# Placing the weights of the last w_o product, the FFN's first sums and a table load elsewhere around an RMS norm

## The chip, the cores and the metric

The kernel runs on one core of one Trainium2 chip. The metric is the device time of one execution in microseconds (us). A core has five engines with a queue each: TensorE (PE: matrix products and transposes, into PSUM), VectorE (DVE), ScalarE (ACT), GpSimd (POOL), and SyncE (SP), which here issues most DMA transfers. An engine takes its instructions in the order in which they were written or scheduled; where one waits, all behind it on that engine wait too.

## The reference

One block of a streaming encoder on 512 tokens of 1024 features, in float32 (the FFN has 2816 inner columns). Only the part from the gated merge to the FFN's start concerns the change:

```python
h = h + (g_a * ya + g_b * yb) @ w_o[l]
hn = rmsnorm(h, norm_ffn_g[l])      # xf * rsqrt(mean(xf * xf) + EPS) * g
gu = hn @ w_ffn_in[l]
g, up = jnp.split(gu, 2, axis=-1)
h = h + (jax.nn.silu(g) * up) @ w_ffn_out[l]
```

## The kernel before, in words

Every float32 operand of a product is split into a high and a low part (`split`, L80: ACT copies the rounded high part, DVE subtracts it for the low part), and a product is three matmuls (`mm3`, L74 to L78: high x high, high x low, low x high). So each weight tile costs a DMA into a raw tile, one ACT and one DVE instruction, before TensorE can use it.

The product with w_o is done by Strassen's scheme (Winograd's form) in seven products of half size, each in two steps u = 0, 1 over the inner dimension (`h_multiply`, L874). Their order is a11 x b11, a12 x b21, s1 x t1, s2 x t2, s4 x b22 (the fifth), s3 x t3, a22 x t4 (the last). The right sides b and t are blocks of w_o and sums of them (the sums were stored in DRAM earlier); `blocks_wo` (L816) loads and splits the two tiles of one side, and `wo_part` (L805) chooses the pool. Weight tiles lie in rings: `wop` has four places of tag `whl`, `wp` four of its own, and the raw tiles use three places of `wp`, taken in turn. A tile that takes a place waits until all readers of the place's tile before it are through; a raw place is free when the DVE half of its split has ended. Before the change t1 and t2 lie in `wp` and all other sides in `wop`, so that t4 takes the places of b22.

The fifth product is done for one tile of 128 tokens after the other. Behind each one stands the norm: `finish_h` (L900) adds the product to h (DVE), squares it with a sum along the row (ACT, then a small reduce on DVE), and `scaled` (L339) takes the root (ACT), the reciprocal (DVE) and scales the row (DVE, tile `xs_ffn`). `turned` (L345) transposes two token tiles at a time on TensorE (`pt_ffn`), and ACT and DVE write the high and low part (`hn`) and a plain copy (`x32`) out of PSUM. hn00 and hn10 are the features of tokens 0 to 255, hn01 and hn11 those of tokens 256 to 511. The first pair of FFN column blocks, fg0 and fu0, is multiplied plainly (`project_part`), first with tokens 0 to 255, then with the rest. All later pairs (fg2, fu2, ...) go through Strassen's scheme as well: `weight_sums` (L159) loads a block's two halves and forms four sums of its quarters on DVE (L173 to L176, tiles s21 and s34), which are then split. For fg2 this is begun ahead: the sums s21 and s34, and the split of s21; the raw halves are loaded a second time for the rest.

The order on TensorE is written out by hand from the first product to the end of fg0 and fu0 with the first tokens (`manual_schedule`). The order on all other engines is set by a scheduler, which follows the order of the code where dependences leave a choice, and its own estimate of when each operand is ready. It puts each DMA where its place becomes free.

Which ACT functions are loaded is a table: a root behind other functions needs a table load in front of it, which is an ACT instruction of its own. L945 takes a root of a constant into `warm` to have the table early.

Of the kernel before, what the change touches and what calls it, by code (L numbers as in the profile page):

```python
# [36 lines left out]
def block_kernel(ctx: ExitStack, tc: tile.TileContext, x, norm_mix_g, w_in, b_merge, rel_table,  # L37
# [42 lines left out]
    def split(hi, lo, src):  # L80

        act.activation(hi, src, AF.Copy)  # L82
        dve.tensor_sub(lo, src, f(hi))  # L83
# [161 lines left out]
    def weights(name, ahead=1):  # L245
        prefetch(index[name] + 1 + ahead)
        return made[index[name]]
# [555 lines left out]
    wo = {}  # L803

    def wo_part(name, src):  # L805

        raw = wp.tile([P, 2, S], F32, tag="raw", bufs=3, name=f"raw_{name}")
        sp.dma_start(out=raw[:], in_=src)
        pl = wp if 4 <= len(wo) < 8 else wop
        hl = pl.tile([P, 2, 2, S], F32R, tag="whl", bufs=4, name=f"whl_{name}")  # L810
        split_pair(hl, raw[:])
        wo[name] = hl
# [31 lines left out]
    for j in range(KT):  # L844
        if j >= 4 and j % 2 == 0:
            blocks_wo(("b11", "b21")[j // 2 - 2])
        py = mm_tile(f"po_ya{j}")
        project(py, weights(f"ya{j - j % 2}"), j % 2, aT)
        dve.scalar_tensor_tensor(ta[j], ta[j], 1.0, py[:], ALU.add, ALU.mult)
        dve.tensor_add(ta[j], ta[j], zB[j])  # L850
        at = lo_half if j % 4 < 2 else slice(0, S)
        split(mT[j][:, 0, at], mT[j][:, 1, at], ta[j][:, at])
        if j % 4 == 3:
            m_sum("s1", j // 4)
            m_split("s1", j // 4)
            for name in ("s2", "s4", "s3"):
                m_sum(name, j // 4)
# [25 lines left out]
    def h_read(half, cc, into, tokens=range(2)):  # L883
        for i in tokens:
            hs = ht[2 * into[0] + i][:, into[1] * S:(into[1] + 1) * S]
            dve.scalar_tensor_tensor(hs, bank_of(2 * half + i, cc)[:], 0.5, hs, ALU.mult, ALU.add)
# [17 lines left out]
    with tc.manual_schedule(engines={mybir.EngineType.PE}):  # L904
        h_multiply("a11", "b11", 1, 0, True)
        for u in range(2):
            m_split("s2", u)
        h_read(1, 0, (0, 0))
        h_multiply("a12", "b21", 0, 0, True)
        for t in range(2):  # L910
            finish_h(t, 0, False)
        for u in range(2):
            m_split("s4", u)
        blocks_wo("t3")
        h_multiply("s1", "t1", 0, 1, True)
        for u in range(2):
            m_split("s3", u)
        h_read(0, 1, (1, 1))
        h_multiply("s2", "t2", 1, 0, False)
        h_read(1, 0, (0, 1))  # L920
        blocks_wo("t4")
    aw_stack.close()
    qk_stack.close()
    rnn_stack.close()
# [17 lines left out]
    def hn_at(k, part, half):  # L942
        return bl[k // 4, half][:, part, k % 4]

    act.activation(warm[:], eps_t[:], AF.Sqrt)  # L945
    weight_sums("fg2", True)
    def project_part(o, name, c, half, ks):
        at = slice(c * P, (c + 1) * P)
        whl = weights(name, 0)
# [5 lines left out]
    ends = range(0, KT // 2), range(KT // 2, KT)  # L955
    with tc.manual_schedule(engines={mybir.EngineType.PE}):
        xs = []
        for t in range(2):
            h_multiply("s4", "b22", 0, 1, False, (t,))
            finish_h(t, 1, True)  # L960
            xs.append(scaled(x32p, ht, hsq, "ffn", t)[0])
        weights("fg0")
        h_multiply("s3", "t3", 1, 0, False, us=(0,))
        h_multiply("s3", "t3", 1, 0, False, (0,), us=(1,))
        for jp in (0, 2):
# [5 lines left out]
        for u, jp in ((0, 4), (1, 6)):  # L971
            h_multiply("a22", "t4", 1, 0, False, (0,), us=(u,))
            turned(xs, jp, gf, hn_at, 0, "ffn", f_at)
        finish_h(2, 0, True)
        xs = [scaled(x32p, ht, hsq, "ffn", 2)[0]]
        h_multiply("a22", "t4", 1, 0, False, (1,))
        finish_h(3, 0, True)
# [2 lines left out]
        for name, c in (("fg0", 0), ("fg0", 1), ("fu0", 0), ("fu0", 1)):  # L980
# [8 lines left out]
            project_part(first[-1], name, c, 0, ends[1])  # L989
            if (name, c) == ("fg0", 1):  # L990
                turned(xs, 4, gf, hn_at, 1, "ffn", f_at)
    wo_stack.close()
    xn_stack.close()

# [299 lines left out]
```

## Time and profile before

| | us |
|---|---|
| median of 3 runs (868.69 to 869.67) | 869.65 |
| profiled execution | 871.49 |
| its span | 869.7 |
| TensorE busy | 851.7 (98%) |
| DVE busy | 632.4 (73%) |
| ACT busy | 505.5 (58%) |
| from the fifth product of w_o (497.8) to the first Strassen product of the FFN (551.4) | 53.6 |
| TensorE idle in 500 to 530 | 6.56 |

All times in the rows are counted from the span's start. In a timeline row the first number is the start, the second the duration, and a bracket at the end names the idle time of the engine ahead of the row and what ended it. A row that stands for several instructions (x2, x8) has their number behind it. [...]

### The profile page before, as it was taken

The numbers are of one execution on the slowest core, as the hardware profiler recorded it, in microseconds if no ns is written. First come the engines' busy times: TensorE is split into PE (matmuls) and PEld (weight loads), VectorE is DVE, ScalarE is ACT, GpSimd is POOL, SyncE is SP. The second block draws the span as 40 slices with busy tenths as digits, with TensorE's granted clock in tenths as the row PEclk, the third lists the DMA queues.
The fourth block names the chain that finished last, engine by engine and source line by source line (L and its number), as shares of the span: only waits on it lengthen the run. The fifth ranks groups of instructions, "written<-read, shape, count | busy, mean of one in ns | idle before, by whom it ended". The sixth has DMA issues, their size and how long they took to land.

```text
span 869.7 us, 13005 instructions
## 1 busy us (share of the span) xinstructions
PE 851.7 (98%) x4896; PEld 746.2 (86%) x4896; DVE 632.4 (73%) x973; ACT 505.5 (58%) x869; POOL 97.8 (11%) x135
## 2 busy tenths in 40 slices
PE   8999999999999999999999979999999999999996
PEld 6977887888888888888888868999999999988885
DVE  5789776646666656566558887899888886498973
ACT  7577687641466666567543474565655655474544
POOL 2013312200122222222200000000000001000011
PEclk9999999999999999999999999999999999999999
DMA  8585323339842223242246450747434333394602
GB/s 270 185 300 170 97 73 107 114 107 348 271 129 65 73 66 92 73 122 62 73 145 205 159 165 30 268 145 277 136 115 129 98 97 94 101 323 138 197 20 96
DMA packets 95838, 124.68 MB, mean 143 GB/s; under 512 B 6432, under 2 KB 71568, under 8 KB 95776
## 3 DMA queue, kind: packets, MB, share of 16 engines
q1 hardware_dynamic: 92096, 116.19, 41.0%
q10 hardware_dynamic: 3680, 7.67, 3.1%
q8 instruction: 38, 0.62, 0.3%
q14 instruction: 24, 0.20, 0.1%
HBM read 109.12 MB, written 14.72 MB: 142 GB/s over the span
## 4 chain that ended last, share of the span: by engine, by line
PE 93%; DMA 2%; DVE 2%; ACT 2%; issue 1%; DVEq 0%; ACTq 0%
PE po_out L78 4%; PE po_out L77 4%; PE po_out L76 4%; PE o L749 2%; PE p_fu L77 2%; PE p_fg L77 2%; PE p_fu L78 2%; PE p_fg L78 2%; PE p_fg L76 2%; PE p_fu L76 2%; PE pT L729 2%; PE po_ga L76 2%; PE po_v L76 2%; PE po_q L76 2%; PE po_ga L78 2%; PE po_k L76 2%
## 5 line engine op out<-in xcount | busy, mean ns | idle before, releaser
L718 POOL TENSOR_SCALAR p<-p,rl 128x128 f32<-128x128 f32 (+1 forms) x64 | 39.6, 637 | 165.4 <-DVE rl L716 165.3
L715 ACT ACTIVATE p<-p,m 128x128 f32<-128x128 f32 (+1 forms) x64 | 35.8, 562 | 14.4 <-DVE m L714 14.4
L1057 POOL TENSOR_TENSOR act_lo<-act,act_hi 128x1024 fp32r<-128x1024 f32 x1 | 2.4, 2427 | 306.4 <-ACT act_hi L1056 306.4
L83 DVE TENSOR_TENSOR pp<-pT,pp 128x384 fp32r<-128x384 f32 (+1 forms) x48 | 27.8, 595 | 9.8 <-ACT pp L82 9.7
L83 DVE TENSOR_TENSOR whl_t<-raw_t,whl_t 128x1024 fp32r<-128x1024 f32 x24 | 29.3, 1219 | 4.1 <-ACT whl_t L82 4.1
L714 DVE CUSTOM_DVE_ANT_0 p<-s,bias 128x128 f32<-128x128 f32 (+1 forms) x64 | 29.2, 483 | 3.9 <-PE s L711 3.8
L83 DVE TENSOR_TENSOR whl_qk<-raw_qk,whl_qk 128x1024 fp32r<-128x1024 f32 x16 | 21.5, 1345 | 11.3 <-ACT whl_qk L82 11.3
L82 ACT ACTIVATE whl_t<-raw_t 128x1024 fp32r<-128x1024 f32 x24 | 25.1, 1049 | 6.8 <-PE po_out L78 4.0
L76 PE MATMUL po_gr<-xnT,whl_gr 128*128 128x512 f32 (+1 forms) x80 | 28.1, 352 | 0.1
L597 DVE TENSOR_TENSOR spillf<-spillf,spillf 128x1024 f32<-128x1024 f32 x16 | 19.5, 1221 | 11.7 <-DMA spillf<-in_w_ffn_out_dram 11.7
L77 PE MATMUL po_xr<-xnT,whl_xr 128*128 128x512 f32 (+1 forms) x80 | 27.8, 353 | 0.1
L77 PE MATMUL po_gr<-xnT,whl_gr 128*128 128x512 f32 (+1 forms) x80 | 27.8, 348 | 0.0
L78 PE MATMUL po_gr<-xnT,whl_gr 128*128 128x512 f32 (+1 forms) x80 | 27.5, 348 | 0.0
L83 DVE TENSOR_TENSOR whl_fg_s<-s_fg,whl_fg_s 128x1024 fp32r<-128x1024 f32 x20 | 24.3, 1222 | 4.3 <-ACT whl_fg_s L82 4.3
L78 PE MATMUL po_xr<-xnT,whl_xr 128*128 128x512 f32 (+1 forms) x80 | 27.4, 347 | 0.0
L76 PE MATMUL po_xr<-xnT,whl_xr 128*128 128x512 f32 (+1 forms) x80 | 26.7, 353 | 0.6 <-ACT xnT L353 0.6
L83 DVE TENSOR_TENSOR whl_b<-raw_b,whl_b 128x1024 fp32r<-128x1024 f32 x18 | 21.9, 1218 | 6.6 <-ACT whl_b L82 6.4
L83 DVE TENSOR_TENSOR whl_fu_s<-s_fu,whl_fu_s 128x1024 fp32r<-128x1024 f32 x20 | 24.3, 1222 | 3.1 <-ACT whl_fu_s L82 3.1
L82 ACT ACTIVATE whl_qk<-raw_qk 128x1024 fp32r<-128x1024 f32 x16 | 16.8, 1052 | 16.0 <-PE po_yb L78 8.8
L82 ACT ACTIVATE whl_b<-raw_b 128x1024 fp32r<-128x1024 f32 x18 | 18.9, 1051 | 12.1 <-DMA raw_b<-in_w_o_dram 11.5
L76 PE MATMUL po_gb<-xnT,whl_gb 128*128 128x512 f32 x64 | 25.1, 393 | 0.5 <-DVE sp_p L452 0.3
L76 PE MATMUL po_ga<-xnT,whl_ga 128*128 128x512 f32 x64 | 25.3, 396 | 0.0
(386 smaller groups left out, 3259.4 us busy)
## 6 DMA issues: line engine op xcount, KB each, us to landing
raw_fg<-in_w_ffn_in_dram SPq DMA_DIRECT2D x24, 512.0 KB, 3.9
raw_fu<-in_w_ffn_in_dram SPq DMA_DIRECT2D x22, 512.0 KB, 3.6
raw_qk<-in_w_in_dram SPq DMA_DIRECT2D x32, 256.0 KB, 3.3
spillf<-in_w_ffn_out_dram SPq DMA_DIRECT2D x16, 512.0 KB, 7.3
sums<-spillf SPq DMA_DIRECT2D x16, 512.0 KB, 4.3
raw_t<-sums SPq DMA_DIRECT2D x16, 512.0 KB, 4.4
raw_b<-in_w_ffn_out_dram SPq DMA_DIRECT2D x12, 512.0 KB, 3.5
raw_xr<-in_w_in_dram SPq DMA_DIRECT2D x8, 512.0 KB, 4.6
```

The lines of the kernel that those rows point to most:

```text
L76: pe.matmul(o, sh, mh, start=start, stop=False, skip_group_check=parts)
L77: pe.matmul(o, sh, ml, start=False, stop=False, skip_group_check=parts)
L78: pe.matmul(o, sl, mh, start=False, stop=stop, skip_group_check=parts)
L82: act.activation(hi, src, AF.Copy)
L83: dve.tensor_sub(lo, src, f(hi))
L597: dve.tensor_sub(out_, a_, b_)
L714: dve.tensor_tensor_reduce(prob[qb][:], scs[qb], bias[:, S - w:S], -1.0, 3e38, ALU.add, ALU.min, nmax[:, qb:qb + 1])
L715: act.activation(prob[qb][:], prob[qb][:], AF.Exp, bias=nmax[:, qb:qb + 1], scale=-1.0, accum_out=lsum[:, qb:qb + 1])
L718: pool.tensor_scalar(prob[qb][:], prob[qb][:], rl[:, qb:qb + 1], 1.0, ALU.mult, ALU.mult)
L729: pe.transpose(pt[:, at * P:(at + 1) * P], prob[qb][:, kb * P:(kb + 1) * P], ident[:])
L749: pe.matmul(po[:, S - n:S], st, pp[i][:, part, lo:lo + n], start=kb == 0 and part == 0, stop=kb == NT - 1 and part == 1)
L1057: (pool if i == 0 else dve).tensor_sub(lo[:], o[:], f(hi[:]))
```

## The change

It makes four edits. The sides t1, t2 and t4 now lie in `wp`, the sides b11, b21, b22 and t3 in `wop`, so that t4 takes the places of t1, fg0 those of t2, and fu0 those of t4. t4 is loaded and split ahead of the read of the fourth product, and fg0 ahead of the fifth product; fu0 is asked for behind the read of the last product's first half, where before both came behind the fifth product. The sums of fg2 are asked for behind the transposes of the second tokens, no longer ahead of the fifth product. And the root that loads the table now depends on the fifth tile of the merged branches (`ta[4]`) and stands behind it.

```diff
@@ wo_part
-        pl = wp if 4 <= len(wo) < 8 else wop
+        pl = wp if name[:2] in ("t1", "t2", "t4") else wop
@@ the merge of the branches, tile j
         split(mT[j][:, 0, at], mT[j][:, 1, at], ta[j][:, at])
+        if j == 4:
+            act.activation(warm[:], ta[4][:, 0:1], AF.Sqrt, scale=0.0, bias=eps_t[:])
         if j % 4 == 3:
@@ the first four products
         h_read(0, 1, (1, 1))
+        blocks_wo("t4")
         h_multiply("s2", "t2", 1, 0, False)
         h_read(1, 0, (0, 1))
-        blocks_wo("t4")
@@ ahead of the fifth product
-    act.activation(warm[:], eps_t[:], AF.Sqrt)
-    weight_sums("fg2", True)
@@ from the fifth product on
         xs = []
+        weights("fg0", 0)
         for t in range(2):
             h_multiply("s4", "b22", 0, 1, False, (t,))
             finish_h(t, 1, True)
             xs.append(scaled(x32p, ht, hsq, "ffn", t)[0])
-        weights("fg0")
@@ behind the first token tile of the last product
         finish_h(2, 0, True)
+        weights("fu0", 0)
         xs = [scaled(x32p, ht, hsq, "ffn", 2)[0]]
@@ fg0 and fu0 with the first tokens
             if (name, c) == ("fg0", 1):
                 turned(xs, 4, gf, hn_at, 1, "ffn", f_at)
+                weight_sums("fg2", True)
```

What the scheduler makes of it is seen in the order of the instructions. The first place is DVE from the read of the fifth product's first token tile (h0) to the reciprocal root of token tile 1 (`rs_ffn1`), before. `hsq` is a row's sum of squares, `rs` its reciprocal root, `xs` the scaled tile:

```order
L886 SCALAR_TENSOR_TENSOR h0_4382<-po_h0_1_4502,h0_4382 128x512
L897 TENSOR_REDUCE hsq0_4622<-hsq2_0_4481 128x1
L83 TENSOR_TENSOR whl_t4_0_4562<-raw_t4_0_4560,whl_t4_0_4562 128x1024
L886 SCALAR_TENSOR_TENSOR h1_4383<-po_h1_1_4509,h1_4383 128x512
L336 RECIPROCAL rs_ffn0_4626<-sd_ffn0_4624 128x1
L83 TENSOR_TENSOR whl_t4_1_4567<-raw_t4_1_4565,whl_t4_1_4567 128x1024
L342 TENSOR_SCALAR xs_ffn0_4628<-h0_4382,rs_ffn0_4626 128x1024
L897 TENSOR_REDUCE hsq1_4645<-hsq2_1_4485 128x1
L173 TENSOR_TENSOR s21_fg2_4596<-raw_fg2_0_4592,raw_fg2_4_4594 128x512
L886 SCALAR_TENSOR_TENSOR h2_4384<-po_h2_0_4422,h2_4384 128x512
L336 RECIPROCAL rs_ffn1_4649<-sd_ffn1_4647 128x1
```

And the same place in the change:

```order
L888 SCALAR_TENSOR_TENSOR h0_4383<-po_h0_1_4503,h0_4383 128x512
L899 TENSOR_REDUCE hsq0_4619<-hsq2_0_4482 128x1
L336 RECIPROCAL rs_ffn0_4623<-sd_ffn0_4621 128x1
L342 TENSOR_SCALAR xs_ffn0_4625<-h0_4383,rs_ffn0_4623 128x1024
L888 SCALAR_TENSOR_TENSOR h1_4384<-po_h1_1_4510,h1_4384 128x512
L175 TENSOR_TENSOR s34_fg2_4870<-raw_fg2_0_4865 128x512
L899 TENSOR_REDUCE hsq1_4642<-hsq2_1_4486 128x1
L336 RECIPROCAL rs_ffn1_4646<-sd_ffn1_4644 128x1
```

The two splits of t4 and the sums s21 of fg2 no longer stand between the norm's rows; one sum, s34 out of fg2's first half, does.

The second place is SP's queue behind t4's second tile, before (raw_fg2_0 and raw_fg2_4 are the two halves of fg2's weights):

```order
L808 DMA raw_t4_1_4565<-sums_o1_3_465 128x1024
L147 DMA raw_fg2_0_4592<-in_w_ffn_in_dram 128x4x256
L147 DMA raw_fg2_4_4594<-in_w_ffn_in_dram 128x4x256
L147 DMA raw_fg0_0_4653<-in_w_ffn_in_dram 128x4x256
L147 DMA raw_fg0_4_4658<-in_w_ffn_in_dram 128x4x256
L147 DMA raw_fu0_0_4663<-in_w_ffn_in_dram 128x4x256
L147 DMA raw_fu0_4_4668<-in_w_ffn_in_dram 128x4x256
L147 DMA raw_fg2_0_4977<-in_w_ffn_in_dram 128x4x256
L147 DMA raw_fu2_0_5106<-in_w_ffn_in_dram 128x4x256
```

And in the change:

```order
L808 DMA raw_t4_1_4540<-sums_o1_3_465 128x1024
L147 DMA raw_fg0_0_4594<-in_w_ffn_in_dram 128x4x256
L147 DMA raw_fg0_4_4599<-in_w_ffn_in_dram 128x4x256
L147 DMA raw_fu0_0_4743<-in_w_ffn_in_dram 128x4x256
L147 DMA raw_fu0_4_4748<-in_w_ffn_in_dram 128x4x256
L147 DMA raw_fg2_0_4865<-in_w_ffn_in_dram 128x4x256
L147 DMA raw_fg2_4_4867<-in_w_ffn_in_dram 128x4x256
L147 DMA raw_fg2_0_4977<-in_w_ffn_in_dram 128x4x256
L147 DMA raw_fu2_0_5106<-in_w_ffn_in_dram 128x4x256
```

fg2's first two transfers move from ahead of fg0's to behind fu0's. By the three raw places in turn, fg2's second half now takes the place of fu0's first half, and so waits for its split.

The third place is DVE from the read of the last product to the scaling of token tile 3, before:

```order
L897 TENSOR_REDUCE hsq2_4764<-hsq2_2_4721 128x1
L886 SCALAR_TENSOR_TENSOR h3_4385<-po_h3_0_4429,h3_4385 128x512
L173 TENSOR_TENSOR s21_fu2_5110<-raw_fu2_0_5106,raw_fu2_4_5108 128x512
L354 SCALAR_TENSOR_TENSOR hn10_4585<-pt_ffn0_6_4750,vc_383,hn10_4585 128x256
L358 TENSOR_SCALAR x32_3_4590<-pt_ffn0_6_4750,vc_383 128x256
L336 RECIPROCAL rs_ffn2_4768<-sd_ffn2_4766 128x1
L174 TENSOR_TENSOR s21_fu2_5110<-s21_fu2_5110,raw_fu2_0_5106 128x512
L897 TENSOR_REDUCE hsq3_4787<-hsq2_3_4724 128x1
L342 TENSOR_SCALAR xs_ffn2_4770<-h2_4384,rs_ffn2_4768 128x1024
L336 RECIPROCAL rs_ffn3_4791<-sd_ffn3_4789 128x1
L342 TENSOR_SCALAR xs_ffn3_4793<-h3_4385,rs_ffn3_4791 128x1024
```

And in the change:

```order
L83 TENSOR_TENSOR whl_fu0_0_4745<-raw_fu0_0_4743,whl_fu0_0_4745 128x1024
L888 SCALAR_TENSOR_TENSOR h3_4386<-po_h3_0_4430,h3_4386 128x512
L354 SCALAR_TENSOR_TENSOR hn10_4586<-pt_ffn0_6_4727,vc_383,hn10_4586 128x256
L358 TENSOR_SCALAR x32_3_4591<-pt_ffn0_6_4727,vc_383 128x256
L336 RECIPROCAL rs_ffn2_4755<-sd_ffn2_4753 128x1
L83 TENSOR_TENSOR whl_fu0_4_4750<-raw_fu0_4_4748,whl_fu0_4_4750 128x1024
L899 TENSOR_REDUCE hsq3_4774<-hsq2_3_4701 128x1
L342 TENSOR_SCALAR xs_ffn2_4757<-h2_4385,rs_ffn2_4755 128x1024
L173 TENSOR_TENSOR s21_fg2_4869<-raw_fg2_0_4865,raw_fg2_4_4867 128x512
L336 RECIPROCAL rs_ffn3_4778<-sd_ffn3_4776 128x1
L174 TENSOR_TENSOR s21_fg2_4869<-s21_fg2_4869,raw_fg2_0_4865 128x512
L342 TENSOR_SCALAR xs_ffn3_4780<-h3_4386,rs_ffn3_4778 128x1024
```

Before, two sums of fu2 (s21_fu2) stand in this stretch and the first of them ahead of both reciprocals; now it is two sums of fg2, the first ahead of the reciprocal of token tile 3 alone, and the second split of fu0 stands in it too.

## The prediction

> **What bounds the kernel now.** I read the page's totals first, then stretches of the span, then the waits of TensorE, then each engine's rows in order of time around them.
>
> ```profile
> PE 851.7 (98%) x4896; PEld 746.2 (86%) x4896; DVE 632.4 (73%) x973; ACT 505.5 (58%) x869; POOL 97.8 (11%) x135
> 490.00:500.00 10.00, 10.00 (x46) 8.29 (x45) 6.34 (x10) 1.52 (x4) 0.00 (x0) 1.00 0.27 91
> 500.00:510.00 10.00, 7.95 (x36) 6.08 (x34) 6.61 (x13) 5.64 (x10) 0.00 (x0) 1.00 0.34 102
> 510.00:520.00 10.00, 7.52 (x31) 5.92 (x32) 9.47 (x15) 8.29 (x16) 0.00 (x0) 0.83 0.72 213
> 520.00:530.00 10.00, 7.97 (x47) 7.26 (x46) 6.98 (x17) 4.86 (x13) 0.00 (x0) 0.88 0.35 106
> 530.00:540.00 10.00, 10.00 (x82) 10.00 (x82) 6.77 (x14) 5.59 (x13) 0.00 (x0) 0.94 0.01 2
> 540.00:550.00 10.00, 10.00 (x86) 10.00 (x84) 10.00 (x16) 7.26 (x11) 0.00 (x0) 1.00 0.18 52
> 550.00:560.00 10.00, 10.00 (x86) 10.00 (x85) 8.52 (x11) 4.34 (x7) 0.00 (x0) 1.00 0.90 316
> 580.00:850.00 270.00, 270.00 (x1872) 253.28 (x1871) 222.77 (x295) 152.56 (x251) 4.96 (x3) 1.00 0.43 141
> ```
>
> Columns: the stretch, its length, then busy time of TensorE, its weight load, DVE, ACT and POOL, the granted clock, the DMA share and GB/s. TensorE has no gap from 490 to 500 or from 530 to 850. Between 500 and 530 it is idle for 2.05 + 2.48 + 2.03 = 6.56 us, and the clock falls to 0.83. While ACT works 1.52 of 10 us and DVE 6.34 just ahead, both are full in the gap. What is won here reaches the end, because everything behind is TensorE's; what is won elsewhere does not.
>
> TensorE's rows, with the wait in brackets:
>
> ```profile
> 503.04 0.39 PE L78 MATMUL po_h<-whl_b,mT 128*128 128x512 f32 x1
> 507.12 0.39 PE L78 MATMUL po_h<-whl_t,mT 128*128 128x512 f32 x1
> 507.75 0.44 PE L349 MATMUL pt_ffn<-ident,xs_ffn 128*128 128x128 f32 x2 [0.24 <-DVE hsq L897]
> 510.76 1.54 PE L349 MATMUL pt_ffn<-ident,xs_ffn 128*128 128x128 f32 x6 [2.58 <-DVE xs_ffn L342]
> 517.48 0.63 PE L349 MATMUL pt_ffn<-ident,xs_ffn 128*128 128x128 f32 x4 [1.57 <-ACT whl_fu L82]
> 527.70 0.58 PE L77 MATMUL po_f<-hn,whl_fg 128*128 128x256 f32 x1 [2.03 <-DVE hn L354]
> 530.43 0.42 PE L77 MATMUL po_f<-hn,whl_fg 128*128 128x256 f32 x1
> 530.64 0.41 PE L78 MATMUL po_f<-hn,whl_fg 128*128 128x256 f32 x1
> 530.85 1.17 PE L349 MATMUL pt_ffn<-ident,xs_ffn 128*128 128x128 f32 x8
> 532.45 0.28 PE L78 MATMUL po_f<-hn,whl_fg 128*128 128x256 f32 x1
> 532.57 0.28 PE L76 MATMUL po_f<-hn,whl_fg 128*128 128x256 f32 x1
> 537.57 0.60 PE L349 MATMUL pt_ffn<-ident,xs_ffn 128*128 128x128 f32 x4
> 537.92 0.36 PE L76 MATMUL po_f<-hn,whl_fu 128*128 128x256 f32 x1
> ```
>
> From 503.04 to 507.12 stand 18 products of 512 columns, one each 0.227 us; four transposes take 0.35 (537.57 to 537.92). Neighbouring 256-column products start 0.21 us apart at 530.5 and 0.12 at 532.5. So the waits of 2.58 and 2.03 us also cost a slow stretch of some 4 us; the one of 1.57 hardly does.
>
> What the norm of token tile 1 waits for stands on DVE and ACT:
>
> ```profile
> 503.24 1.23 DVE L83 TENSOR_TENSOR whl_t<-raw_t,whl_t 128x1024 fp32r<-128x1024 f32 x1 [0.80 <-ACT whl_t L82]
> 504.38 0.68 DVE L886 SCALAR_TENSOR_TENSOR h<-po_h,h 128x512 f32<-128x512 f32 x1
> 507.61 0.15 DVE L897 TENSOR_REDUCE hsq<-hsq 128x1 f32<-128x2 f32 x1
> 508.09 0.69 DVE L173 TENSOR_TENSOR s_fg<-raw_fg,raw_fg 128x512 f32<-128x512 f32 x1 [0.34 <-DMA raw_fg<-in_w_ffn_in_dram]
> 509.30 0.15 DVE L336 RECIPROCAL rs_ffn<-sd_ffn 128x1 f32<-128x1 f32 x1
> 509.96 0.75 DVE L342 TENSOR_SCALAR xs_ffn<-h,rs_ffn 128x1024 f32<-128x1024 f32 x1
> 520.56 0.48 DVE L354 SCALAR_TENSOR_TENSOR hn<-pt_ffn,vc,hn 128x256 fp32r<-128x256 f32 x1
> 526.56 0.69 DVE L173 TENSOR_TENSOR s_fu<-raw_fu,raw_fu 128x512 f32<-128x512 f32 x1 [2.79 <-DMA raw_fu<-in_w_ffn_in_dram]
> 529.53 0.75 DVE L342 TENSOR_SCALAR xs_ffn<-h,rs_ffn 128x1024 f32<-128x1024 f32 x1
> 502.16 1.04 ACT L82 ACTIVATE whl_t<-raw_t 128x1024 fp32r<-128x1024 f32 x1
> 503.22 1.28 ACT L334 ACT_TABLE_LOAD   x1
> 505.67 0.61 ACT L894 ACTIVATE hj<-h 128x512 f32<-128x512 f32 x1
> 506.19 0.19 ACT L894 ACTIVATION_READ_ACCUMULATOR hj<-h 128x1 f32 x1
> 507.79 0.29 ACT L334 ACTIVATE sd_ffn<-hsq,eps_t 128x1 f32<-128x1 f32 x1 [1.41 <-DVE hsq L897]
> ```
>
> The fifth product ends at 503.04 + 0.39 = 503.4, but its norm is ready only at 509.96 + 0.75 = 510.7, since the splits of t4, the load of the root's table, and the FFN's sums stand between its links. Likewise the wait at 525.4 to 527.7 is DVE held by a sum whose weights had not landed.
>
> **The change part by part.** *Table load.* Its 1.28 us go behind the split of the fifth branch tile. The nearest rows are there:
>
> ```profile
> 465.46 1.99 ACT L82 ACTIVATE whl_t<-raw_t 128x1024 fp32r<-128x1024 f32 x2
> 472.27 0.63 ACT L82 ACTIVATE mT<-za 128x512 fp32r<-128x512 f32 x1 [2.71 <-DVE za L850]
> 504.49 3.57 DMA raw_fg<-in_w_ffn_in_dram
> DMA to landing us min/median/max: 5.8/7.4/9.0
> ```
>
> Two splits of t1, used from 487 on, come 1.28 + 0.29 = 1.6 us later; ACT's wait of 2.71 us at 472 takes that up. I cost it at nothing. Without that cover it would be 1.6.
>
> *t4's weights in the other ring.* t4 now takes the places of t1, free when the third product ends, and no longer those of b22, which the fifth product still reads. Its two splits (1.04 on ACT, 1.23 on DVE each) and fg0's two go into DVE's idle 3.66 us and ACT's idle 8.48 us before 500. Four DVE rows are 4.9 us, more than 3.66, but the four sums of fg2 leave that stretch or its end too. fg0's last split: t4's first ends on DVE at about 494.2 (the third product's end, 503.4 - 48 x 0.227 = 492.5, a read of 0.68, the split's 1.23), its raw place takes fg0's second half, landed 3.57 later (the chain's row) at 497.8; t2's place is free at 503.4 - 24 x 0.227 = 498.0; 1.04 and 1.23 with their hand-overs end at 500.4, before the first token tile of the fifth product is through, 503.4 - 12 x 0.227 = 500.7. Nothing on the path; a slip of 1 us there is worth less than 1 us, since tile 0's scaling has until 507.4.
>
> *Token tile 1.* Its read of the product starts at 503.7, behind tile 0's scaling: 0.68, square 0.61 + 0.19, reduce 0.15, root 0.29, reciprocal 0.15, scaling 0.75, and some 0.2 of handing over: 506.7. One sum of fg2 (0.69) stands between, under ACT's square; it waits for a transfer that follows fg0's last split at 500.4 and takes 3.57 (the chain's row): 504.0. So the transposes follow the product's rows at 507.4 without a wait. This removes 2.58 + 0.24.
>
> *Second pair of transposes.* fu0's splits leave this place, so the wait of 1.57 falls to what the reads of the first transposes need. Behind 508.1 DVE does h2's and h3's reads and five rows of 0.48 in turn with ACT's: 511.4 against TensorE's 510.8, a wait of 0.6.
>
> *fu0 and fg2.* fu0 now takes t4's places, so its split waits for the last product. TensorE is there through with t4's first half at 507.4 + 0.7 (8 transposes) + 18 products at 0.227 + 0.6 + 2 x 0.35 + 6 more = 514.9; ACT 1.04 and DVE 1.23 end at 517.3. Only that frees the place for fg2's second half, which lands 3.57 later: 520.9. And the sum that reads it stands on DVE ahead of the reciprocal of token tile 3. This is the change's new wait: behind it stand the reciprocal 0.15, a sum 0.67 and the scaling 0.75, with the sum itself 0.69: 523.1. TensorE has by then only fg0's first 36 products (0.12 each, 4.3 us) from 516.1, so it waits from 520.4 to 523.1, some 2.6 us. Bounds: 1.1 if the transfer hid entirely (517.3 + a read 0.68 + two rows of 0.48 + fu0's second split 1.23 + 0.15 + 0.29 + 0.15 + 0.75 = 521.5), 8.0 if it took the longest landing shown here, 9.0. I take 2.6, the nearest row being one transfer alone.
>
> *The sum.* The transposes of the second half start at 523.1 instead of 530.85: 7.75 us less. A wait of 2.6 us sets a slow stretch behind it, as the waits of 2.58 and 2.03 do now; of today's (527.70 to about 532) three quarters already lie ahead of 530.85. So I give back 14 products at 0.21 - 0.12 and slower transposes, 1.6 us, less the 0.4 that lies behind today: 1.2. Leaves 6.5. For the FFN's start, where DVE has the moved sums and a split to do beside a full 10 us, I give back 0.5: **6.0 us**.
>
> The row of the clock is 0.83 in 510 to 520, after a wait of 2.58. [...]
>
> The profiled execution took 871.49 us around its span of 869.7, 1.84 above the median of 869.65. The rows are of that one execution and its gap is no outlier in them, so the difference is taken off the median: 869.65 - 6.0 = **863.7 us**.
>
> **The rivals.** *DVE decides the FFN's start.* From 530 to 560 DVE works 6.77 + 10.00 + 8.52 = 25.3 of 30 us. The change puts two sums, a split and part of fg2's sums, 2.9 us, behind the last scaling. If all its idle 4.7 stays too, DVE gains 7.75 - 2.9 - 0.5 = 4.3: 865.3. For it speaks the 10.00 between 540 and 550; against it that this idle time is waiting on things that come earlier now. *The clock stays up* behind the 2.6 us wait, as behind the 1.57: 862.5. *Given back among the products.* The scheduler has re-sorted DVE and ACT in the later blocks as well. If each of the ten pairs cost TensorE 0.6, 6 us would be gone: 869.7. Against it: 270 of 270 busy with DVE at 222.77. *Slower: sums waiting for weights hold the norm.* Should transfers of fg2 take 9.0 rather than 3.57, token tile 3's reciprocal stands 5.4 behind; and fu2's sum, which now stands ahead of a split of the normed tile, repeats it for about 3.5 more. 6.0 - 5.4 - 3.5 is a loss of 2.9: 872.6. It decides from a landing of some 7.2 us on (6.0 = 1.65 x 3.6 later). Against it: by my chain the next transfer is issued only after fu0's second split, some 2.6 us later, while the slow landings fell where the DMA engines were 0.72 and 0.90 busy. *The table load fails to move* (today's early root stands near ACT's start and helps nothing): 1.28 us then falls on token tile 0's root, whose scaling would end at 505.1, still before 507.4; no other time follows.
>
> **How the numbers follow.** Forecast 0.55; DVE decides 0.22; clock stays up 0.10; given back 0.07; slower 0.06. Under 0.2% (1.7 us) this kernel's runs tell no change, so faster is 0.55 + 0.22 + 0.10 = 0.87, same 0.07, slower 0.06. The range goes from 861.8 (the clock's case with its 0.5 back for the FFN's start, and a little more) to 867.2 (a landing of 5.8 and DVE's case together: 863.7 + 2.2 + about 1.3).
>
> **What would show it.** Right: no table load near 503; transposes at about 507.4 with no wait over 0.3; one wait of TensorE of 2 to 3 us near 520 to 523, put down to the scaling of token tile 3 or a sum of fg2, with DVE waiting for the DMA of fg2 just ahead; TensorE's idle time between 500 and 530 near 3.3 us instead of 6.56. Wrong: a wait at 507 that remains (then fg2's first half lands late), waits among 545 to 565 (then DVE decides), or TensorE below 270 in its long stretch.

## The result, and the profile after

The changed kernel takes 866.89 us (median of 8 runs, 866.41 to 868.03); the kernel before, timed beside it, 869.3 (8 runs, 868.69 to 869.67). The ratio is 0.9974, with a 95% interval of 0.9963 to 0.9985: faster by 2.4 us, where 6.0 were forecast. The profiled execution took 866.91 us around a span of 865.1, so it is a typical one.

The page's totals and the stretches of the span (columns as in the prediction):

```profile
PE 849.9 (98%) x4896; PEld 743.7 (86%) x4896; DVE 632.7 (73%) x973; ACT 505.1 (58%) x869; POOL 97.8 (11%) x135
490.00:500.00 10.00, 10.00 (x46) 8.27 (x45) 9.95 (x13) 5.66 (x8) 0.00 (x0) 1.00 0.66 203
500.00:510.00 10.00, 10.00 (x50) 8.35 (x49) 6.21 (x14) 4.15 (x13) 0.00 (x0) 1.00 0.34 101
520.00:530.00 10.00, 8.11 (x64) 7.32 (x63) 7.88 (x17) 5.80 (x11) 0.00 (x0) 1.00 0.59 178
540.00:550.00 10.00, 9.16 (x75) 8.76 (x73) 9.74 (x14) 8.57 (x13) 0.00 (x0) 1.00 0.71 216
550.00:560.00 10.00, 8.84 (x71) 8.63 (x72) 8.51 (x11) 2.27 (x7) 0.00 (x0) 1.00 1.01 385
580.00:845.00 265.00, 265.00 (x1830) 248.21 (x1830) 217.14 (x285) 150.48 (x247) 4.95 (x3) 1.00 0.43 142
```

DVE and ACT now do in 490 to 500 what they had idle time for (9.95 and 5.66 us against 6.34 and 1.52), TensorE has no gap left in 500 to 510, and the clock stays at 1.00. But two stretches that were full before, 540 to 560, now have gaps of 0.84 + 1.16 = 2.0 us. TensorE's rows say where:

```profile
507.25 1.04 PE L349 MATMUL pt_ffn<-ident,xs_ffn 128*128 128x128 f32 x8
511.38 0.63 PE L349 MATMUL pt_ffn<-ident,xs_ffn 128*128 128x128 f32 x4 [0.33 <-DVE x L358]
521.01 0.41 PE L349 MATMUL pt_ffn<-ident,xs_ffn 128*128 128x128 f32 x2
523.16 0.88 PE L349 MATMUL pt_ffn<-ident,xs_ffn 128*128 128x128 f32 x6 [1.74 <-DVE xs_ffn L342]
543.94 0.28 PE L76 MATMUL p_fg<-hn,whl_fg_a 128*128 128x256 f32 x1
549.38 0.39 PE L76 MATMUL q_fg<-hn,whl_fg_a 128*128 128x256 f32 x1 [0.72 <-ACT whl_fg_a L82]
550.17 0.39 PE L76 MATMUL p_fg<-bt,whl_fg_s 128*128 128x256 f32 x1 [0.29 <-ACT keepa_fg L277]
559.57 0.38 PE L76 MATMUL q_fg<-hn,whl_fg_s 128*128 128x256 f32 x1 [0.99 <-ACT keepb_fg L277]
```

The transposes of the second tokens, at 530.85 before, start at 523.16 (7.69 us earlier; the first two, of token tile 2, run at 521.01). The first Strassen product (p_fg<-hn), at 551.44 before, starts at 543.94 (7.50 earlier). The end is 869.7 - 865.1 = 4.6 us earlier: 2.9 us are given back behind that product, 2.0 of them in its three waits and the rest in the rows around them. DVE and ACT around them:

```profile
499.14 1.22 DVE L83 TENSOR_TENSOR whl_fg<-raw_fg,whl_fg 128x1024 fp32r<-128x1024 f32 x1
506.12 0.76 DVE L342 TENSOR_SCALAR xs_ffn<-h,rs_ffn 128x1024 f32<-128x1024 f32 x1
521.02 0.69 DVE L173 TENSOR_TENSOR s_fg<-raw_fg,raw_fg 128x512 f32<-128x512 f32 x1 [0.16 <-DMA raw_fg<-in_w_ffn_in_dram]
528.46 0.69 DVE L173 TENSOR_TENSOR s_fu<-raw_fu,raw_fu 128x512 f32<-128x512 f32 x1 [1.45 <-DMA raw_fu<-in_w_ffn_in_dram]
551.57 1.28 DVE L83 TENSOR_TENSOR whl_fg_a<-raw_fg,whl_fg_a 128x512 fp32r<-128x512 f32 x2
465.88 1.28 ACT L854 ACT_TABLE_LOAD   x1
473.83 0.63 ACT L82 ACTIVATE mT<-za 128x512 fp32r<-128x512 f32 x1 [2.38 <-DVE za L850]
554.59 0.39 ACT L277 ACTIVATE keepb_fg<-p_fg 128x256 f32<-128x256 f32 x1 [2.30 <-PE p_fg L78]
558.62 0.63 ACT L82 ACTIVATE whl_fg_a<-raw_fg 128x512 fp32r<-128x512 f32 x1 [3.64 <-DMA raw_fg<-in_w_ffn_in_dram]
559.15 0.36 ACT L277 ACTIVATE keepb_fg<-q_fg 128x256 f32<-128x256 f32 x1
```

fg2's second half lands at 521.0, as forecast (520.9). What was not forecast is the chain behind it: fu2's transfer waits for the places that fg2's sums free, lands at 528.4, and from then on DVE has no more than 1 us of idle time up to 552.85. Its last row there frees the place for the next pair's weights, whose transfer is issued at 552.88 and lands at 558.6; and ACT has the split of these weights in its queue ahead of the read of q_fg (keepb_fg), so that ACT stands for 3.64 us and TensorE behind it for 0.99.

### The profile page after: what moved, and what is told of

Same layout as the page of the kernel before. It is cut to its first block, busy times and chain, and to the rows that moved or that the text cites. A ratio compares the mean times of both kernels' runs of the same rounds, so it can differ in the third digit from the quotient of the medians.

```text
span 865.1 us, 13011 instructions
## 1 busy us (share of the span) xinstructions
PE 849.9 (98%) x4896; PEld 743.7 (86%) x4896; DVE 632.7 (73%) x973; ACT 505.1 (58%) x869; POOL 97.8 (11%) x135
## 4 chain that ended last, share of the span: by engine, by line
PE 88%; DVE 4%; issue 3%; DMA 2%; ACT 2%; POOL 0%; ACTq 0%; DVEq 0%
PE po_out L76 4%; PE po_out L77 4%; PE po_out L78 4%; PE o L749 2%; PE p_fu L76 2%; PE p_fu L78 2%; PE p_fu L77 2%; PE pT L729 2%; PE p_fg L78 2%; PE p_fg L77 2%; PE p_fg L76 2%; PE po_ga L76 2%; PE po_v L76 2%; PE po_q L76 2%; PE po_ga L78 2%
```

## The experiments

One number sorts all kernels: the time from the first Strassen product of the FFN to the end of the span. Both times are read in each kernel's own profiled execution; the median and the ratio are of timed runs.

| kernel | median us | ratio to before (95%) | first Strassen product | from there to the end |
|---|---|---|---|---|
| before, the execution that the prediction read | | | 551.44 | 318.3 |
| before, again | 869.44 | 1.0004 (0.9995 to 1.0013) | 548.61 | 318.3 |
| before + early table | 868.96 | 0.9995 (0.9987 to 1.0004) | 549.02 | 318.3 |
| before + moved sums | 868.74 | 0.9996 (0.9988 to 1.0005) | 548.13 | 318.3 |
| **the change** | 866.89 | 0.9974 (0.9963 to 0.9985) | 543.94 | **321.2** |
| the change, again | 866.97 | 0.9972 (0.9961 to 0.9983) | 545.12 | **320.3** |
| the change without the early table | 867.28 | 0.9975 (0.9966 to 0.9984) | 545.40 | **320.1** |
| the change without the moved sums or the table (rings and places alone) | 864.51 | 0.9945 (0.9932 to 0.9957) | 544.21 | 318.3 |
| **the change without the moved sums** | 863.67 | 0.9941 (0.9929 to 0.9954) | 543.75 | 318.7 |
| the change, sums between fg0 and fu0 | 864.04 | 0.9945 (0.9933 to 0.9958) | 543.98 | 318.3 |
| the change, fu0 in b22's places | 864.91 | 0.9949 (0.9936 to 0.9963) | 544.64 | 318.3 |
| the change, fu0 in t3's places | 865.58 | 0.9956 (0.9944 to 0.9969) | 544.46 | 318.2 |
| the same, sums at their old place | 864.92 | 0.9955 (0.9941 to 0.9969) | 544.87 | 318.2 |
| the change, an early split on GpSimd | 865.00 | 0.9956 (0.9943 to 0.9968) | 544.93 | 318.3 |
| the change, a later split on GpSimd | 865.27 | 0.9958 (0.9945 to 0.9972) | 544.75 | 318.7 |

In the last column 318.3 is the time that TensorE needs when nothing waits there. 1.8 to 2.9 us above it are the change, its second profile and the change without the early table; all others give back nothing there, or 0.4 us.

For the change, again (its second profile) a wait of 1.2 to 2.2 us near 523, waits of 1.5 to 2.5 us in sum at 549 to 560 and a full clock throughout had been expected. The wait near 523 is there (1.91 us), but the later ones come to 0.29 + 0.88 = 1.17, and the clock falls to 0.66 in 523 to 528. The loss recurs; its parts differ from one execution to the next.

### Was the profile that the prediction read a typical one?

The kernel before, unchanged, with a second profile.

> The kernel before, unchanged. Theory A (the profiled execution of the kernel before, 871.49 us, was itself some 2.2 us above the kernel's median of 869.3, so its rows overstate what can be won): this run's times lie at 869.3 +- 0.5, the ratio is 1.000, and where a profiled execution comes out near 869.3 its rows lack about 2 us that the first profile had: either the slow clock behind one of the two waits (510 to 530 at 1.00 instead of 0.83 and 0.88) or part of the idle 6.56 us in 500 to 530. Rival B (the profiled execution is typical in its rows, the difference lies elsewhere in the span): a new profile shows 6.5 us idle and 0.83 and 0.88 again, also when its time is 869.3.

Measured: 869.44 us (868.38 to 872.09); the profiled execution took 868.68, with a span of 866.9 against 869.7. Its stretches 510 to 530, and the rows that answer to those of the two waits in the prediction:

```profile
510.00:520.00 10.00, 9.09 (x33) 7.09 (x34) 9.54 (x14) 8.31 (x14) 0.00 (x0) 0.67 0.73 218
520.00:530.00 10.00, 9.33 (x65) 8.27 (x65) 7.65 (x19) 6.44 (x16) 0.00 (x0) 1.00 0.30 99
```

```profile
510.54 1.54 PE L349 MATMUL pt_ffn<-ident,xs_ffn 128*128 128x128 f32 x6 [2.43 <-DVE xs_ffn L342]
525.68 0.39 PE L77 MATMUL po_f<-hn,whl_fg 128*128 128x256 f32 x1 [0.31 <-DVE hn L354]
524.54 0.69 DVE L173 TENSOR_TENSOR s_fu<-raw_fu,raw_fu 128x512 f32<-128x512 f32 x1 [1.07 <-DMA raw_fu<-in_w_ffn_in_dram]
```

The wait of 2.58 us is there again (2.43), with its slow clock. The wait of 2.03 us is 0.31, and 520 to 530 runs at 1.00: fu2's transfer landed at 524.5 and not at 526.5. The wait of 1.57 us at 517 is 0.37 there, but the transposes behind it start only 0.13 us earlier (517.35), since the clock ahead of them is slower (0.67 in 510 to 520, for 0.83). So the difference of 869.7 - 866.9 = 2.8 us of span lies at the second wait and its slow stretch, which this execution lacks. Theory A holds: the rows of the first profile promised a gain that the median does not have to give. Executions as long as the first come again, but seldom: of the 81 others that were timed of the kernel before, 4 took more than 870.5 us. Whether they have the same wait was not profiled.

### The early table load

Alone, added to the kernel before:

```diff
+        if j == 4:
+            act.activation(warm[:], ta[4][:, 0:1], AF.Sqrt, scale=0.0, bias=eps_t[:])
...
-    act.activation(warm[:], eps_t[:], AF.Sqrt)
```

> The kernel before with the early table load alone (the root now depends on the fifth tile of the merged branches). The prediction's reading (the load of 1.28 us is one of three things between the links of the norm; DVE, with two splits and a sum, decides): token tile 1's scaling starts less than 0.5 us earlier than 509.96, time 869.0 to 869.3, ratio above 0.999. Rival (the load is what holds token tile 0's root and all DVE rows behind it): the scaling starts 1.2 to 1.3 us earlier, time about 868.0, ratio 0.9985.

And taken out of the change (no early root at all):

> The changed kernel with no early root at all, so that the table's load falls on token tile 0's root behind the fifth product. The prediction's reading (the load of 1.28 us is hidden there too, since tile 0's scaling ends at 505.1 and TensorE needs it at 507.4): 866.5 to 867.2, no wait over 0.3 at 507. Rival (the rows of token tile 1 stand behind those of tile 0 on ACT and DVE, so that tile 1's scaling ends 1.28 us later, about 508.1, where its transposes are due at about 507.6): a wait of 0.3 to 0.9 us at 507 to 508, time 867.2 to 868.0.

Measured: 868.96 us alone, and 867.28 for the change without it (866.97 for the change beside it): no difference that these runs can tell. In the first, the load is gone from 503 and token tile 1's scaling starts at 509.60 instead of 509.96 in the first profile of the kernel before and 509.74 in the second, since a sum ahead of it still waits for its weights:

```profile
507.73 0.69 DVE L173 TENSOR_TENSOR s_fg<-raw_fg,raw_fg 128x512 f32<-128x512 f32 x1 [1.09 <-DMA raw_fg<-in_w_ffn_in_dram]
509.60 0.74 DVE L342 TENSOR_SCALAR xs_ffn<-h,rs_ffn 128x1024 f32<-128x1024 f32 x1
```

In the second, the load stands in front of token tile 0's root at 502.10, token tile 1's scaling ends at 507.59 instead of 506.88, and TensorE is some 0.3 us later behind the transposes, as the rival said at its lower end. In these two pairs the load is worth 0 to 0.3 us.

### The moved sums, alone and taken out

Alone, added to the kernel before:

```diff
-    weight_sums("fg2", True)
...
                 turned(xs, 4, gf, hn_at, 1, "ffn", f_at)
+                weight_sums("fg2", True)
```

> The kernel before with the sums of fg2 asked for behind the transposes of the second tokens, and nothing else. Theory A (the late sums are what costs at the FFN's start, since DVE and ACT have them and their splits to do besides a full stretch): the wait of 2.03 us near 526 goes or shrinks because no sum waits for its transfer there, and 1.5 to 3 us come back as waits behind the first Strassen product of the FFN; time 867.5 to 869.5. Rival (the sums' place costs nothing later): the whole wait of 2.03 us and part of the 2.58 are won, time 865.5 to 867.

Measured: 868.74 us, no difference. The wait of 2.0 us near 526 was not there, but it was not there in the second profile of the kernel before either. At 508 the scheduler filled the place of the sums with the splits of fu0, and token tile 1's scaling came at 510.83, later than with the sums:

```profile
507.58 1.21 DVE L83 TENSOR_TENSOR whl_fu<-raw_fu,whl_fu 128x1024 fp32r<-128x1024 f32 x1
509.69 1.23 DVE L83 TENSOR_TENSOR whl_fu<-raw_fu,whl_fu 128x1024 fp32r<-128x1024 f32 x1 [0.23 <-ACT whl_fu L82]
510.83 0.75 DVE L342 TENSOR_SCALAR xs_ffn<-h,rs_ffn 128x1024 f32<-128x1024 f32 x1
```

The time lies in theory A's range, but not by its mechanism: nothing came back behind the first Strassen product (318.3), and nothing was won ahead of it, since TensorE's wait for token tile 1's scaling grew to 3.55 us (ahead of 511.63). Alone, the edit says nothing about the theories.

Rings and places of t4, fg0 and fu0 alone, without the moved sums and the early table:

> The changed kernel's rings and its places for t4, fg0 and fu0, but fg2's sums and the early root where they were before the change. Theory A (late transfers behind fu0's split are what the change gave back; here fg2's sums are loaded ahead of fg0 and only fu2's transfers come late): the wait at 508 to 510 is under 1.5 us, no waits over 0.5 us at 549 to 560; time 865 to 867. Rival (sums and a split of fg2 between the norm's links, with the table's load, cost as much as t4's splits did): the wait at 508 is 2 us or more with a slow stretch behind it, time 868 to 869.

And the change with only the sums put back:

```diff
+    weight_sums("fg2", True)
     def project_part(o, name, c, half, ks):
...
                 turned(xs, 4, gf, hn_at, 1, "ffn", f_at)
-                weight_sums("fg2", True)
```

> The changed kernel with one edit undone: fg2's sums are asked for ahead of the fifth product again; the rings, the places of t4, fg0 and fu0, and the early table load stay. Theory A (moving the sums is the part of the change that loses: it puts fg2's second half behind fu0's split in the queue of transfers and four sums and a split more on DVE at the FFN's start): the wait of 1.7 to 1.9 us near 523 falls below 0.5, no waits at 549 to 560, time 863.7 to 864.6, that is 2.4 to 3.3 us faster than the changed kernel. Rival (the early load and the moved sums only pay together, so that with the sums back at the norm the wait at 507 to 510 returns): 865.5 to 867.

Measured: 864.51 and 863.67 us, 4.8 and 5.3 us faster than the kernel before beside them (the first 0.5 us below theory A's range, the second at the lower end of its own). The second is the fastest of all, some 3 us faster than the whole change (0.9941 against 0.9972 to 0.9974). Its rows on TensorE and DVE:

```profile
507.37 1.18 PE L349 MATMUL pt_ffn<-ident,xs_ffn 128*128 128x128 f32 x8
522.05 0.87 PE L349 MATMUL pt_ffn<-ident,xs_ffn 128*128 128x128 f32 x6 [0.36 <-DVE xs_ffn L342]
525.07 0.39 PE L77 MATMUL po_f<-hn,whl_fg 128*128 128x256 f32 x1 [0.48 <-DVE hn L354]
499.70 0.69 DVE L176 TENSOR_TENSOR s_fg<-raw_fg,s_fg 128x512 f32<-128x512 f32 x1
521.24 0.75 DVE L342 TENSOR_SCALAR xs_ffn<-h,rs_ffn 128x1024 f32<-128x1024 f32 x1
523.93 0.69 DVE L173 TENSOR_TENSOR s_fu<-raw_fu,raw_fu 128x512 f32<-128x512 f32 x1 [1.93 <-DMA raw_fu<-in_w_ffn_in_dram]
```

With t4's splits out of the way, the four sums of fg2 fit into DVE's rows before 500.4 and hold nothing: the first tokens' transposes run at 507.37 without a wait. The wait of 1.74 us before the second tokens' transposes shrinks to 0.36, fu2's weights land at 523.9 instead of 528.4, and nothing waits at 549 to 560. So the moved sums lose some 3 us in the change, as theory A said. In the first profile of the change nearly all of that lies behind the first Strassen product (543.94 against 543.75 ahead of it, 321.2 against 318.7 behind it); in the second 1.4 us lie ahead and 1.5 behind.

The two kernels differ in the early table load alone. Without it TensorE waits 0.21 and 0.42 us ahead of 507.32 and 508.19, with it there is no such wait. The gains differ by 0.5 us, which is inside their intervals.

Does it matter whether fg2 comes before or behind fg0? Sums asked for behind fg0, ahead of fu0:

> The changed kernel with fg2's sums asked for behind fg0 and ahead of the fifth product's loop, so that its transfers stand behind fg0's and ahead of fu0's. Theory A (what costs is that fg2's second half waits for fu0's split; ahead of fu0 it does not matter whether fg0 or fg2 comes first): as with the sums at their old place, 863.7 to 865, no waits at 549 to 560. Rival (four sums and a split of fg2, now between the rows of the norm of the first tokens, hold token tile 1's scaling): a wait of 1 us or more at 507 to 510, 865.5 to 867.

Measured: 864.04 us, not to be told from the old place. It is enough that fg2's transfers stand ahead of fu0's.

### fu0 in other places

If it is fu0's split that holds everything up, because it waits for the last product to free t4's place, then fu0 should be given another place.

```diff
-        pl = wp if name[:2] in ("t1", "t2", "t4") else wop
+        pl = wp if name[:3] in ("t1_", "t2_", "b22") else wop
...
```

(t3, t4 and b22 are then loaded behind the first, second and third product, and fu0 is asked for behind the second token tile's norm):

> The changed kernel, but t4 lies in the ring of b11 and b21 and b22 in that of t1 and t2, so that fu0 takes the places of b22, which are free at about 503.4 instead of 515; fu0 is asked for behind the second token tile's norm. Theory A (what the change gave back is the chain: fu0's split waits for the last product, so fg2's and fu2's transfers land late, so DVE's sums and ACT's splits wait at 528 and 558 and TensorE at 523, 549, 550 and 560, together about 4.5 us): the wait of 1.74 us at 523 falls below 0.6, DVE's wait of 1.45 us for fu2 at 528 goes, and of the 2.0 us of waits at 549 to 560 at least 1 goes; time 863.5 to 865. Rival B (the waits at 549 to 560 come from the amount of work that DVE and ACT have in 530 to 560, not from late transfers): the wait at 523 goes and comes back at 545 to 560; time 866 to 867. Slower: fu0's splits stand between the links of the norm of tokens 256 to 511; 867.5.

Measured: 864.91 us, inside theory A's range. No wait is left at 520 to 560. But the scheduler, finding the place free at 503, put both of fu0's splits ahead of token tile 1's scaling, and the old wait is back at 507 to 510 with a slow clock (0.94 granted in 500 to 530, 1.00 in the change):

```profile
503.82 1.22 DVE L83 TENSOR_TENSOR whl_fu<-raw_fu,whl_fu 128x1024 fp32r<-128x1024 f32 x1
505.61 1.22 DVE L83 TENSOR_TENSOR whl_fu<-raw_fu,whl_fu 128x1024 fp32r<-128x1024 f32 x1
509.07 0.75 DVE L342 TENSOR_SCALAR xs_ffn<-h,rs_ffn 128x1024 f32<-128x1024 f32 x1
509.87 1.54 PE L349 MATMUL pt_ffn<-ident,xs_ffn 128*128 128x128 f32 x6 [1.82 <-DVE xs_ffn L342]
```

A place that becomes free between these two times is t3's (506 and 511; t4 is then loaded ahead of t3):

```diff
-        pl = wp if name[:2] in ("t1", "t2", "t4") else wop
+        pl = wp if name[:2] in ("t1", "t2", "t3") else wop
...
-        blocks_wo("t3")
+        blocks_wo("t4")
...
-        blocks_wo("t4")
+        blocks_wo("t3")
```

> The changed kernel, but the ring of t1 and t2 takes t3 instead of t4, and t4 is loaded ahead of t3: so fg0 takes t2's places as now and fu0 takes t3's, free at about 506.1 and 510.8, behind token tile 1's scaling and well ahead of the last product's end at 515. Theory A (late transfers behind fu0's split are what the change gave back; the kernel with fu0 in b22's places lost 4.3 us at 507 to 513 only since fu0's splits stood between the norm's links): no wait over 0.5 us at 507, none over 0.6 at 511, none over 0.5 at 520 to 523 nor at 549 to 560, the clock at 1.00 throughout; time 861.5 to 863.5, the fastest of all. Rival B (the work itself is too much for DVE and ACT in 500 to 560, and the waits only move): 864.5 to 866.

Measured: 865.58 us (864.52 to 866.58; the profiled execution is the fastest of these). The waits at 507 and at 549 to 560 are gone, as theory A said, but a new one of 1.61 us stands in between. Ahead of the reads of the transposes DVE now has two sums of fg2 (0.69 and 0.68 us, the first with a wait of 0.41 for fg2's second half) and fu0's second split between them:

```profile
515.12 0.63 PE L349 MATMUL pt_ffn<-ident,xs_ffn 128*128 128x128 f32 x4 [1.61 <-DVE x L358]
511.76 0.69 DVE L173 TENSOR_TENSOR s_fg<-raw_fg,raw_fg 128x512 f32<-128x512 f32 x1 [0.41 <-DMA raw_fg<-in_w_ffn_in_dram]
512.37 1.22 DVE L83 TENSOR_TENSOR whl_fu<-raw_fu,whl_fu 128x1024 fp32r<-128x1024 f32 x1
```

So the time fell into rival B's range, and a wait moved, as rival B said; what moved it is three rows of DVE ahead of the reads and not the work in 500 to 560 as a whole. Why the median is 1.1 us above the profiled execution is not shown. The same with the sums back at their old place:

> The changed kernel with fg2's sums at their old place and t3 instead of t4 in the ring of t1 and t2, so that fu0 takes t3's places and its split no longer waits for the last product. Theory A (after fg2's sums, fu2's late transfer, 1.9 us of DVE's idle time near 523 with the sums back, is the next thing that costs; it follows fu0's second split): waits of TensorE at 521 to 526 under 0.4 us in sum instead of about 1.1; but fu0's first split now stands ahead of token tile 1's reciprocal, which costs up to 1.2 at 507 to 509. Time 863 to 865. Rival B (no gain is left there): 865 to 866.

Measured: 864.92 us, inside theory A's range. No wait at 521 to 526, as said, but 2.29 us at 510, since fu0's first split stands ahead of token tile 1's reciprocal. The price was put at 1.2 at most; the wait alone is nearly twice that, and a slow clock follows it (0.83 in 510 to 520). A fourth raw place, which might free the transfers without moving any split, was not tried.

### What gives back behind the first Strassen product?

A row of DVE was given to GpSimd in each of two kernels, in one a row ahead of fu2's landing at 528.4 and in the other one behind it, to tell the late landing from the amount of work on DVE and from the order on ACT. The first of the two edits (the other gives GpSimd the split of s34 likewise):

```diff
-        dve.tensor_sub(lo, src, f(hi))
+        (by or dve).tensor_sub(lo, src, f(hi))
...
-            split(o[:, :, 0], o[:, :, 1], s21[:])
+            split(o[:, :, 0], o[:, :, 1], s21[:], pool)
```

> The changed kernel with one DVE row given to GpSimd: the low half of the split of fg2's s21 (1.22 us on DVE at 523.6, ahead of its wait of 1.45 us for fu2's transfer at 528). Theory A (what gives the gain back behind the first Strassen product is set by fu2's late transfer: DVE is full without a gap from its landing at 528.5 to 552.9, so work taken off ahead of it only makes the wait for the transfer longer): DVE's wait for raw_fu grows or stays, the stretch from the first Strassen product to the end stays above 319.5 us (321.2 and 320.3 in the two profiles of the changed kernel, 318.3 where nothing waits there), time 866 to 867.2. Theory B (the sum of DVE's work between 520 and 553 decides): that stretch gets 1.2 us shorter, time 865.3 to 866.

> The changed kernel with another DVE row given to GpSimd: the low half of the split of fg2's s34 (1.22 us on DVE at 534.0, behind fu2's transfer). Theory A (DVE is the limit from fu2's landing at 528.5 to 552.9, and every row taken off there counts; ACT's wait of 3.64 us for raw_fg at 558.6 follows it, since DVE's split frees the place of that transfer): the stretch from the first Strassen product to the end falls by about 1.2 us or more, to 319 to 320, time 865.4 to 866. Theory B (ACT's order decides, its split for the next pair standing ahead of the read of keepb): the waits at 549 and 550 stay at 1.0 in sum and only the one at 559.6 goes if ACT's rows change places; time 865.7 to 866.2 with the waits of 549 to 551 still there.

Measured: 865.00 and 865.27 us, each faster than any range that was named for it. One row of 1.2 us brings back about 2 us and more behind the first Strassen product (318.3 and 318.7, for 321.2 and 320.3). Theory A of the first falls, since a row taken off ahead of the landing was to change nothing. But it isn't the amount either. In the first:

```profile
528.49 0.69 DVE L173 TENSOR_TENSOR s_fu<-raw_fu,raw_fu 128x512 f32<-128x512 f32 x1 [0.70 <-DMA raw_fu<-in_w_ffn_in_dram]
556.65 0.39 ACT L277 ACTIVATE keepb_fg<-p_fg 128x256 f32<-128x256 f32 x1 [0.49 <-PE p_fg L78]
558.26 1.15 ACT L82 ACTIVATE whl_fg_a<-raw_fg 128x512 fp32r<-128x512 f32 x2 [1.22 <-DMA raw_fg<-in_w_ffn_in_dram]
```

And in the second:

```profile
551.24 1.29 DVE L83 TENSOR_TENSOR whl_fg_a<-raw_fg,whl_fg_a 128x512 fp32r<-128x512 f32 x2
555.27 0.38 ACT L277 ACTIVATE keepb_fg<-q_fg 128x256 f32<-128x256 f32 x1 [2.31 <-PE q_fg L78]
556.66 0.38 ACT L277 ACTIVATE keepb_fg<-p_fg 128x256 f32<-128x256 f32 x1 [0.49 <-PE p_fg L78]
558.83 1.15 ACT L82 ACTIVATE whl_fg_a<-raw_fg 128x512 fp32r<-128x512 f32 x2 [1.79 <-DMA raw_fg<-in_w_ffn_in_dram]
535.67 1.19 DVE L1022 TENSOR_TENSOR sum_t<-x,sum_t 128x512 f32<-128x512 f32 x1
533.81 2.50 POOL L83 TENSOR_TENSOR whl_fg_s<-s_fg,whl_fg_s 128x1024 fp32r<-128x1024 f32 x1 [109.33 <-ACT whl_fg_s L82]
```

fu2 lands as late as in the change (528.4), DVE ends its run only 0.3 us earlier in the second (552.53 for 552.85), and the next pair's weights land no earlier (558.8 for 558.6). What differs is the order on two engines. The scheduler, given other costs, now has both of ACT's reads (keepb_fg) ahead of the split that waits for these weights, with q_fg's read as the first. And TensorE's order is another too. In the change the second product into p_fg (p_fg<-bt, at 550.17) stands ahead of ten products of q_fu, and so right behind the read of p_fg that it needs (keepa_fg); in both kernels here it stands behind them. The three profiles that give back 1.8 us or more all have the change's order on both engines, and the twelve others all have the other one.

The waits of TensorE at 550 and 559.6 are gone with these orders. They are 0.29 and 0.75 to 0.99 us long. In the second profile of the change and in the change without the early table they are the only ones there, and TensorE ends 2.0 and 1.8 us late behind the first product (320.3 and 320.1 for 318.3), with the rows around them counted in. The wait of 0.72 us at 549.4 stands only in the profile in which the clock stayed up; where TensorE came later by a slow stretch (0.66 granted in 523 to 528 in the second profile, 0.71 without the early table), it was not there. So the late landing makes the wait of ACT's split possible, and the order of the rows hands it on to TensorE. That the orders do it is read from these rows. No run changed an order by itself, so what ACT's order costs and what TensorE's does is open.

## Why the prediction was wrong

Forecast 863.7 us, measured 866.89. The sign was right and the time lies inside the range, but the gain was 2.4 us and not 6.0. By its own steps:

- *Table load at no cost:* right in the cost, wrong in what covers it. ACT's idle time of 2.71 us ahead of mT's split was to take up the 1.6 us, but 2.38 of it is still there: DVE waits for the split of t1 too (1.51 us, ahead of 468.45), so mT's split itself comes 1.56 us later (473.83 for 472.27). TensorE reaches the first product with w_o no later all the same (475.96 for 476.07).
- *t4's and fg0's splits before 500:* right. fg0's last split ends at 499.14 + 1.22 = 500.36 (500.4 said).
- *Token tile 1:* right. Its scaling ends at 506.88 (506.7 said), and the transposes run at 507.25 without a wait.
- *Second pair of transposes:* 0.33 us, 0.6 said.
- *fu0's late split, fg2's late landing, a wait up to 523.1:* right in mechanism and time. DVE waits for fg2 at 521.02, the transposes start at 523.16. The wait is 1.74 and not 2.6 us, since TensorE had products up to 520.9 and not 520.4, and then ran token tile 2's two transposes (521.01).
- *1.2 us for a slow clock behind that wait:* paid in the second profile of the change (0.66 granted in 523 to 528), not in the first (1.00), where the rival *the clock stays up* held. The second execution had its first Strassen product 1.18 us later, 0.19 of it by the longer wait, and ended only 0.3 later, since the wait of 0.72 at 549.4 was not there.
- *0.5 us for the FFN's start:* **this step failed.** It was 2.9 us in the first and 2.0 in the second profile. The prediction had looked up to token tile 3's scaling and not beyond: that fu2's transfers stand behind fg2's in the same three places, and that the scheduler would set ACT's and TensorE's rows of the first Strassen pair anew. Two rivals came close to it. *DVE decides* gave 3.4 us back there by way of DVE's amount of work, and said to look for waits among 545 to 565, where they are. *Sums waiting for weights* named the sum of fu2 ahead of a split of the normed tile; it waited 1.45 us, not 3.5.
- *"The rows are of that one execution and its gap is no outlier in them, so the difference is taken off the median":* **this step failed.** The profiled execution was 871.49 - 869.3 = 2.2 us above the median, and the second profile shows where: it lacks the wait of 2.03 us (0.31 there) and the slow stretch behind it. Its first Strassen product starts at 548.61, so that against it the change is 4.67 us ahead there and not 7.50. A sum that takes away a wait must not take it from runs that do not have it.

Put together: the span fell by 4.6 us against the profiled execution; 4.6 - 2.2 = 2.4 is the gain in the median. Of the 3.6 us that are missing, 2.2 are the execution, 2.9 - 0.5 = 2.4 the FFN's start, less the 1.2 charged for the clock and not paid there; that is 3.4, and 0.2 lie between 7.75 and 7.50.

A wait of some 2 us was followed by a slow stretch in both kernels: one of 2.03 us in the kernel before (0.66 granted in 527.70 to 532.70) and one of 1.91 in the second profile of the change (0.66 in 523 to 528).

With the sums left at their old place the change takes 863.67 us, the time that was forecast; but by other terms than the forecast's, so that is no support for it.

## What to carry to other kernels

A profile is one execution: when it lies off the median by as much as a term of the sum, take a second profile before any wait in it is counted as a gain. When a load is moved back in a queue of shared places, follow every transfer behind it to the last one that moves, not only to the first wait that it makes. And undo each edit of a bundle by itself: here the rings and the new places together won 4.8 us, the table load nothing that could be told, and the sums lost 3.

## What the runs showed of the hardware that was not expected

Whether a slow clock follows a wait of TensorE isn't set by the length of the wait alone. In the change, its first profile, the wait ahead of 523.16 is 1.74 us; with the later split on GpSimd it is 1.75, ahead of 522.97. The stretch 523 to 528 of the first, and of the second:

```profile
523.00:528.00 5.00, 4.82 (x37) 4.45 (x38) 3.50 (x7) 3.02 (x7) 0.00 (x0) 1.00 0.75 219
```

```profile
523.00:528.00 5.00, 5.00 (x30) 5.00 (x31) 3.32 (x6) 2.82 (x7) 0.00 (x0) 0.66 0.69 211
```

Full clock and 37 instructions in the one, 0.66 and 30 in the other. Of TensorE's other waits in 500 to 530, that of 1.57 us in the first profile of the kernel before had no slow clock behind it (1.00 granted in 517.48 to 522.48), nor had 1.61 with fu0 in t3's places (1.00 over 500 to 530). These longer ones had one: 1.91 in the second profile of the change (0.66 in 523 to 528), 1.93 without the early table (0.71 there), 2.03 and 2.58 in the first profile before (0.66 in 527.70 to 532.70 and 0.67 in 510.76 to 515.76), 2.29 with fu0 in t3's places and the sums at their old place (0.83 in 510 to 520), 2.43 in the second profile before (0.67 in 510 to 520) and 3.55 with the moved sums alone (0.89 over 500 to 530). In between either happens: 1.74 had none, while 1.75, 1.77 with the early split on GpSimd (0.66 in 523 to 528) and 1.82 with fu0 in b22's places (0.94 over 500 to 530) had one. What else decides it is not shown.

GpSimd took 2.37 and 2.50 us for the low half of a split that takes DVE 1.22. While it ran at 533.81 to 536.31 (with the later split on GpSimd), one sum on DVE took 1.19 us (535.67) instead of the 0.68 of its neighbours.
